# First expert of a mixture-of-experts stage: slots dealt to its tiles in turns, their read issued after one weight split, its transposes moved into the first step

## The chip, the cores and the metric

The kernel runs on one core of one Trainium2 chip. The metric is the device time of one execution in microseconds. A profiled execution also gives a span, from its first to its last instruction.

## The reference, cut to what matters

One transformer layer for 1024 tokens of 1024 columns: an attention mixer, then a mixture of 32 experts of which each token takes four. The part that the change touches:

```python
top_logits, top_e = lax.top_k(logits, TOP_K)           # 4 of 32 experts for each token
slot_tok = jnp.full((n_slots,), T).at[dest].set(flat_tok[order])
slot_w = jnp.zeros((n_slots,)).at[dest].set(top_w.reshape(-1)[order])
...
gu = xe @ w_gu[e] + b_gu[e]                            # xe: the tokens of expert e, 1024 -> 2048
x_glu = jnp.minimum(gu[:, :D_FF], SWIGLU_LIMIT)
x_lin = jnp.clip(gu[:, D_FF:], -SWIGLU_LIMIT, SWIGLU_LIMIT)
act = (x_lin + 1) * (x_glu * jax.nn.sigmoid(SWIGLU_ALPHA * x_glu))
return act @ w_dn[e] + b_dn[e]                         # 1024 -> 1024
...
y = jnp.zeros((T + 1, D)).at[slot_tok].add(yb * slot_w[:, None])
```

## The kernel before

The mixer ends with a router. For every token tile it writes pairs of (token, weight) into a DRAM table `slots_d` with indirect DMAs (L1295, issued by GpSimd). Each expert has a stretch of that table, and its slots lie one after the other.

The experts are then ranked by how many tokens they have, and the expert of rank r gets a fixed capacity `CAPS[r]`: 304, 280, 256, 224, 216, 208, 200, 184, 184, 176, 160, 160, 152, 144, 144, 136, then 128 fourteen times, and 64 twice. `positions()` puts the wide ones (capacity over 128) on even positions p = 0, 2, ... 30 in falling order, and the others between them. Position 0 has 304 slots, position 2 has 280, position 30 has 136, and position 31 has 128.

An expert at position p is worked on so. `slots(p)` (L1530) reads its part of `slots_d` into SBUF. `gather(p)` (L1546, GpSimd) fetches the token rows of 4 KB from DRAM, one indirect DMA for each tile of up to 128 slots. `xtr(p)` queues, for each tile and each half of the columns, a small chain `one`: four TensorE transposes (L1601), a rounded copy by ScalarE (`put_hi`, L1585) and the remainder by VectorE (`put_lo`, L1588). The weights come in pieces of 128x1024 (512 KB, `load`, L1493, on SyncE's queue). ScalarE and VectorE split each piece into a high and a low part (`split_hi` L1505, `split_lo` L1514). Steps "U" (four for the up projection) and "D" (two for the down projection) of four pieces each do the matmuls. Behind the last D step each tile of results is added to DRAM `f_d` with an accumulating indirect DMA (`scatter`, L1841, GpSimd). All of them add to the same `f_d`, so each waits until the one before it has landed.

Buffers: six for raw pieces, eight high parts, seven low parts, three for gathered tiles (`xg`), two PSUM tiles for transposes (`t5`). The steps follow one list, `steps`. Between pieces `slot()` runs: it advances the queued chains (`hot`, `cold`), then splits and loads one further piece. `need` advances chains until the halves that a step wants are done. Ahead of the first step, `prepare(0)` queues the transposes of position 0, a loop drains all of them, and only then the remaining splits and the steps follow. `prepare(p)` also reads the slots of p + 2 and queues the gather of p + 1, so GpSimd's queue holds gathers and scatters in one order.

Of the kernel before, what the change touches and what calls it, by code (L numbers as in the profile page):

```python
# [18 lines left out]
P = 128  # L19
# [7 lines left out]
def f(ap):  # L27
    return ap.bitcast(F32)
# [938 lines left out]
STRIDE = 1152  # L967
# [474 lines left out]
class Moe2(Tail):  # L1442
    def moe(self):
        nc, A, tc = self.nc, self.A, self.tc
# [18 lines left out]
        for p in range(NE):  # L1463
            c = caps[posr[p]]
# [3 lines left out]
        def ereg(eng, p):  # L1468
            r = posr[p]
            if (eng, p) not in regs:  # L1470
                regs[eng, p] = getattr(nc, eng).value_load(self.erow[0:1, r:r + 1], min_val=0, max_val=31)
            return regs[eng, p]
# [12 lines left out]
        def load(n=1, eng="sync"):  # L1485
            for _ in range(n):
                if st["l"] >= len(pieces):
                    return
                k, p, j, q = pieces[st["l"]]
                e = ereg(eng, p)  # L1490
                r = rawp.tile([P, 1024], F32, name="raw5")
                src = A["w_gu" if k == "U" else "w_dn"]
                getattr(nc, eng).dma_start(r, src[ds(e, 1), j * 4 + q].rearrange("a p c -> p (a c)"))  # L1493
                raws[st["l"]] = r
                st["l"] += 1

        def split_hi(n=1):
            for _ in range(n):
                i = st["h"]
                if i >= len(pieces):  # L1500
                    return
                while i not in raws:
                    load()
                his[pieces[i]] = hi = hip.tile([P, 1024], F32R, name="hi5")
                ACT.activation(hi, raws[i], AF.Copy)  # L1505
                st["h"] += 1

        def split_lo(n=1):
            for _ in range(n):
                i = st["s"]  # L1510
                if i >= len(pieces):
                    return
                los[pieces[i]] = lo = lop.tile([P, 1024], F32R, name="lo5")
                V.tensor_tensor(out=lo, in0=raws.pop(i), in1=f(his[pieces[i]]), op=ALU.subtract)  # L1514
                st["s"] += 1
# [3 lines left out]
        todo = {}  # L1519

        def tiles(p):
            c = caps[posr[p]]
            return [(a, min(P, c - a)) for a in range(0, c, P)]

        def slots(p, eng="sync"):
            if p >= NE:
                return
            e, nt = ereg(eng, p), len(tiles(p))
            sl = xgp.tile([P, 3, 2], I32, name="slot", bufs=8)
            getattr(nc, eng).dma_start(sl[:, :nt], self.slots_d[ds(e * STRIDE, nt * P), :].rearrange("(a p) c -> p a c", p=P))  # L1530
            SL[p] = [sl[:, i] for i in range(nt)]

        def columns(p):

            if p < NE and mode[p] == "T":
                b = xgp.tile([P, 24], F32, name="bcol", bufs=3)
                nc.sync.dma_start(b, A["b_col"][ds(ereg("sync", p), 1)].rearrange("a p c -> p (a c)"))
                BC[p] = b

        def gather(p):  # L1540
            if p >= NE:
                return
            XG[p] = []
            for (a, n), sl in zip(tiles(p), SL[p]):
                xg = xgp.tile([P, D], F32, name="xg")
                G.indirect_dma_start(out=xg[:n], out_offset=None, in_=self.h2_d,  # L1546
                                     in_offset=bass.IndirectOffsetOnAxis(ap=sl[:n, 0:1], axis=0))
                XG[p].append(xg)
# [10 lines left out]
        chains = deque()  # L1559
        hot, cold = deque(), deque()  # L1560

        def start(g):
            if next(g, chains) is not chains:
                chains.append(g)

        def advance():
            for _ in range(len(chains)):
                start(chains.popleft())
            q = hot or cold
            if q:  # L1570
                start(q.popleft())
# [19 lines left out]
        def xtr(p):  # L1591

            if p >= NE:
                return
            X[p], off = xalloc(p, "x")
            x = X[p]

            def one(a, n, xg, g):
                ps = tps.tile([P, 4, P], F32, name="t5")
                for i in range(4):  # L1600
                    T.transpose(ps[:, i, :n], xg[:n, (g * 4 + i) * P:(g * 4 + i + 1) * P], self.ident[:n, :n])  # L1601
                put_hi(ps[:, :, :n], g * 4, 4, a, n, x)
                yield
                put_lo(ps[:, :, :n], g * 4, 4, a, n, x, off)
                if mode[p] == "S" and n < 64:
                    G.memset(f(x[:, g * 4:g * 4 + 4, n:64]), 0.0)
                    G.memset(f(x[:, g * 4:g * 4 + 4, 64 + n:P]), 0.0)
                todo["U", p, g] -= 1

            ts = list(zip(tiles(p), XG.pop(p)))  # L1610
            for g in range(2):
                todo["U", p, g] = len(ts)
                for (a, n), xg in ts:
                    cold.append(one(a, n, xg, g))
            if mode[p] != "T":
                oh = wk.tile([P, P], F32R, name="oneh", bufs=2)
                G.memset(f(oh[64:P]), 0.0)
                V.tensor_copy(oh[0:64], self.R[:, posr[p]:posr[p] + 1].to_broadcast([64, P]))
                if mode[p] == "S":
                    V.tensor_copy(oh[0:64, 64:P], self.zeros[:64, 0:64])  # L1620
                OH[p] = oh
# [222 lines left out]
        def prepare(p):  # L1844

            if p >= NE:
                return
            slots(p + 2)
            columns(p + 2)
            xtr(p)  # L1850

            def then():
                gather(p + 1)
                return
                yield
            cold.append(then())
# [8 lines left out]
        for i in range(3):  # L1865
            cs = slice(i * D, i * D + D)
            ACT.activation(bhl[0:64, cs], rb[:64, cs], AF.Copy)
            V.tensor_tensor(out=bhl[32:64, cs], in0=rb[32:64, cs], in1=f(bhl[32:64, cs]), op=ALU.subtract)
        for i in range(4):
            split_hi()  # L1870
            split_lo()
            load()
            if i == 2:
                slots(0, "scalar")
                gather(0)
                slots(1, "scalar")
                G.memset(f(bhl[64:P]), 0.0)
        prepare(0)
        while cold or chains:
            advance()  # L1880
        split_hi(4)
        split_lo(3)
        for k, p, j in steps:
            (step_U if k == "U" else step_D)(p, j)
            if (k, p, j) == ("U", 0, 0):
# [187 lines left out]
```

## Time and profile before

| what | value |
|---|---|
| median of three runs | 2809.72 us (2807.43 to 2810.39) |
| the profiled execution's own time | 2805.38 us |
| its span | 2803.8 us |
| TensorE busy | 2667.9 us, 95% of the span |
| VectorE, ScalarE, GpSimd busy | 1959.0, 1591.8, 569.2 us |
| mean busy share of the DMA engines, expert stage | 0.67 to 0.93 by stretch |

The profiled execution spends 1.6 us outside its span, and it is 4.3 us below the median of the runs. Times in rows are microseconds from the start of the span. The expert stage begins at about 1162 and ends at about 2769.

### The profile page before, as it was taken

The numbers are of one execution on the slowest core, as the hardware profiler recorded it, in microseconds if no ns is written. First come the engines' busy times: TensorE is split into PE (matmuls) and PEld (weight loads), VectorE is DVE, ScalarE is ACT, GpSimd is POOL, SyncE is SP. The second block draws the span as 40 slices with busy tenths as digits, with TensorE's granted clock in tenths as the row PEclk, the third lists the DMA queues.
The fourth block names the chain that finished last, engine by engine and source line by source line (L and its number), as shares of the span: only waits on it lengthen the run. The fifth ranks groups of instructions, "written<-read, shape, count | busy, mean of one in ns | idle before, by whom it ended". The sixth has DMA issues, their size and how long they took to land. (4 is left out here: it accounts for less than half of the span.)

```text
span 2803.8 us, 44121 instructions
## 1 busy us (share of the span) xinstructions
PE 2667.9 (95%) x15564; PEld 2232.2 (80%) x15564; DVE 1959.0 (70%) x3148; ACT 1591.8 (57%) x2486; POOL 569.2 (20%) x492
## 2 busy tenths in 40 slices
PE   6999999999999999599999999999999999999993
PEld 4788887455677778499988899999989898999892
DVE  3722332777777546577877887888888888888895
ACT  3421211555577325356666666777777777777773
POOL 2310001665644232401010011011001100111001
PEclk9999999999999999699999999999999999999996
DMA  6225560502132343467787888898889889998896
GB/s 237 73 95 178 186 201 38 169 15 50 40 69 64 113 145 128 156 220 234 261 275 246 278 291 266 276 295 295 267 292 307 292 285 308 315 309 298 304 312 224
DMA packets 196608, 589.37 MB, mean 210 GB/s; under 512 B 49168, under 2 KB 55904, under 8 KB 196240
## 3 DMA queue, kind: packets, MB, share of 16 engines
q1 hardware_dynamic: 173424, 521.43, 55.5%
q0 software_dynamic: 19376, 63.70, 8.4%
q8 instruction: 123, 2.02, 0.3%
q10 hardware_dynamic: 3584, 1.40, 0.2%
q14 instruction: 101, 0.83, 0.1%
HBM read 528.75 MB, written 59.00 MB: 210 GB/s over the span
## 5 line engine op out<-in xcount | busy, mean ns | idle before, releaser
L1514 DVE TENSOR_TENSOR lo<-raw,hi 128x1024 fp32r<-128x1024 f32 x768 | 920.4, 1221 | 166.6 <-ACT hi L1505 67.9
L1505 ACT ACTIVATE hi<-raw 128x1024 fp32r<-128x1024 f32 x768 | 800.7, 1055 | 187.4 <-PE g L1669 85.6
L1669 PE MATMUL g<-xT,hi 128*128 128x320 f32 (+10 forms) x1792 | 518.6, 331 | 0.0
L1670 PE MATMUL g<-xT,lo 128*128 128x256 f32 x1792 | 483.7, 280 | 0.0
L1669 PEld LDWEIGHTS g<-xT,hi 128*128 128x128 f32 x1792 | 336.6, 188 | 10.9
L1670 PEld LDWEIGHTS g<-xT,lo 128*128 128x128 f32 x1792 | 338.4, 189 | 2.6
L1841 POOL DMA_INDIRECT f_d<-y,slot x34 | 61.1, 1797 | 1243.5 <-ACT y L1829 1103.9
L1669 PE MATMUL g<-aT,hi 128*128 128x288 f32 (+10 forms) x896 | 260.4, 333 | 0.0
L1670 PE MATMUL g<-aT,lo 128*128 128x256 f32 x896 | 241.8, 280 | 0.0
L1645 PE MATMUL g<-hi,xN 128*128 128x512 f32 x512 | 204.3, 399 | 0.0
L1646 PE MATMUL g<-lo,xN 128*128 128x512 f32 x512 | 203.3, 397 | 0.0
L174 DVE TENSOR_TENSOR wlo<-raw,whi 128x1024 fp32r<-128x1024 f32 x33 | 42.1, 1289 | 219.0 <-ACT whi L173 218.8
L1644 PE MATMUL g<-hi,xN 128*128 128x512 f32 x448 | 183.0, 408 | 0.0
L1669 PEld LDWEIGHTS g<-aT,hi 128*128 128x128 f32 x896 | 168.3, 188 | 5.2
L1670 PEld LDWEIGHTS g<-aT,lo 128*128 128x128 f32 x896 | 169.1, 189 | 0.7
L859 ACT ACTIVATE p<-S 128x512 f32<-128x512 f32 x160 | 94.2, 596 | 103.8 <-PE S L858 99.0
L613 DVE TENSOR_REDUCE mn<-S 128x1 f32<-128x512 f32 x180 | 100.9, 595 | 66.4 <-PE S L612 66.0
L400 PE MATMUL mm<-hTh,whi 128*128 128x512 f32 (+1 forms) x416 | 123.7, 385 | 1.7 <-ACT whi L173 1.7
L400 PE MATMUL mm<-hTh,wlo 128*128 128x512 f32 (+1 forms) x416 | 123.2, 383 | 0.0
L400 PE MATMUL mm<-hTl,whi 128*128 128x512 f32 (+1 forms) x416 | 123.0, 383 | 0.0
L1646 PEld LDWEIGHTS g<-lo,xN 128*128 128x128 f32 x512 | 96.8, 189 | 22.7
L1645 PEld LDWEIGHTS g<-hi,xN 128*128 128x128 f32 x512 | 97.0, 189 | 19.3
(414 smaller groups left out, 5807.9 us busy)
## 6 DMA issues: line engine op xcount, KB each, us to landing
raw<-in_w_gu_dram SPq DMA_DIRECT2D x512, 512.0 KB, 5.2
raw<-in_w_dn_dram SPq DMA_DIRECT2D x256, 512.0 KB, 4.4
raw<-in_w_mod_dram SPq DMA_DIRECT2D x40, 512.0 KB, 4.3
raw<-in_w_in_dram SPq DMA_DIRECT2D x34, 512.0 KB, 4.7
x<-in_x_dram SPq DMA_DIRECT2D x16, 512.0 KB, 4.9
sig_d<-stg POOLq DMA_DIRECT2D x16, 512.0 KB, 2.9
sig<-sig_d SPq DMA_DIRECT2D x8, 1024.0 KB, 5.0
kraw<-ka_d SPq DMA_DIRECT2D x16, 320.0 KB, 6.9
```

Of the source, the lines that this page charges most:

```text
L174: (G if i == 0 else V).tensor_tensor(out=lo, in0=r, in1=f(hi), op=ALU.subtract)
L400: T.matmul(ps[:, :n], w[:, ks], h[:, k, a:a + n], start=k == 0 and pi == 0, stop=k == KT - 1 and pi == 2)
L613: nc.vector.tensor_reduce(out=u.mn[:, i, j:j + 1], in_=ps[:, :n], op=ALU.min, axis=AX.X)
L859: nc.scalar.activation(u.p[t // 2][:, t % 2 * 512:t % 2 * 512 + 512], ps, AF.Exp, scale=-1.0)
L1505: ACT.activation(hi, raws[i], AF.Copy)
L1514: V.tensor_tensor(out=lo, in0=raws.pop(i), in1=f(his[pieces[i]]), op=ALU.subtract)
L1644: T.matmul(ps[:m], x[:, kk, P:P + m], hi[:, cs], start=False, stop=False)
L1645: T.matmul(ps[:m], x[:, kk, :m], hi[:, cs], start=False, stop=False)
L1646: T.matmul(ps[:m], x[:, kk, :m], lo[:, cs], start=False, stop=kk == 7)
L1669: T.matmul(ps[:, :2 * c], hi[:, cs], x[:, kk, :], start=first, stop=False)
L1670: T.matmul(ps[:, :256], lo[:, cs], x[:, kk, :256], start=False, stop=last)
L1841: G.indirect_dma_start(out=self.f_d, out_offset=bass.IndirectOffsetOnAxis(ap=SL[p][xi][:n, 0:1], axis=0), in_=Y[p][xi][:n], in_offset=None ...
```

## The change

It makes three edits.

1. `tiles(p)` no longer cuts the capacity c into tiles of 128 and a rest, but into t = ceil(c / 128) tiles whose sizes differ by one at most. 304 slots were 128, 128, 48 and become 102, 101, 101. 280 were 128, 128, 24 and become 94, 93, 93. The other wide ones were 128 and a rest and become two halves: 128 (as before), 112, 108, 104, 100, 92, 92, 88, 80, 80, 76, 72, 72 and 68.
2. `slots(p)` deals slots to the tiles in turns: slot s goes to partition s // t of tile s % t. For each partition the read then is one run of 8 t bytes instead of t runs of 8 bytes.
3. Ahead of the first step the loop runs seven times instead of four. The slot read, the gather of position 0 and the slot read of position 1 are issued after the first split instead of after the third. An eighth `split_hi` stands ahead of `prepare(0)`, and the drain is gone, so that the transposes of position 0 run where the first step asks for them.

```diff
         def tiles(p):
+
             c = caps[posr[p]]
-            return [(a, min(P, c - a)) for a in range(0, c, P)]
+            t = -(-c // P)
+            ns = [(c - i + t - 1) // t for i in range(t)]
+            return [(sum(ns[:i]), ns[i]) for i in range(t)]

         def slots(p, eng="sync"):
             if p >= NE:
                 return
-            e, nt = ereg(eng, p), len(tiles(p))
+            e, nt, n = ereg(eng, p), len(tiles(p)), tiles(p)[0][1]
             sl = xgp.tile([P, 3, 2], I32, name="slot", bufs=8)
-            getattr(nc, eng).dma_start(sl[:, :nt], self.slots_d[ds(e * STRIDE, nt * P), :].rearrange("(a p) c -> p a c", p=P))
+            getattr(nc, eng).dma_start(sl[:n, :nt].rearrange("p a c -> p (a c)"),
+                                       self.slots_d[ds(e * STRIDE, n * nt), :].rearrange("(p a) c -> p (a c)", a=nt))
             SL[p] = [sl[:, i] for i in range(nt)]
...
-        for i in range(4):
+        for i in range(7):
             split_hi()
             split_lo()
             load()
-            if i == 2:
+            if i == 0:
                 slots(0, "scalar")
                 gather(0)
                 slots(1, "scalar")
                 G.memset(f(bhl[64:P]), 0.0)
+        split_hi()
         prepare(0)
-        while cold or chains:
-            advance()
-        split_hi(4)
-        split_lo(3)
         for k, p, j in steps:
```

## Rows read from the trace of the kernel before

**Rows 1.** Busy time by stretch: PE, PEld, DVE, ACT, POOL, PE clock, DMA share, GB/s
```profile
1200.00:1300.00 100.00, 97.90 (x649) 92.18 (x649) 75.02 (x104) 56.83 (x76) 2.33 (x2) 0.98 0.67 214
...
2400.00:2600.00 200.00, 199.70 (x1308) 181.71 (x1307) 174.12 (x237) 150.58 (x225) 25.92 (x20) 1.00 0.93 310
```

**Rows 2.** Timeline, start of the expert stage: start, duration, engine, line, instruction, [idle before]
```profile
1165.26 1.04 POOL L1295 DMA_INDIRECT slots_d<-data,sl  x1 [0.22 <-issue]
...
1167.28 1.06 ACT L1505 ACTIVATE hi<-raw 128x1024 fp32r<-128x1024 f32 x1 [1.73 <-DMA raw<-in_w_gu_dram]
...
1171.57 1.62 ACTq L1530 DMA_DIRECT2D slot<-slots_d  x2
...
1173.24 1.06 ACT L1505 ACTIVATE hi<-raw 128x1024 fp32r<-128x1024 f32 x1 [1.60 <-DVE lo L1514]
...
1179.19 0.99 POOL L1546 DMA_INDIRECT xg<-h_d,slot  x1 [12.90 <-DMA slot<-slots_d]
```

**Rows 3.** Landing: the last table write of 1165.26, then position 0's slot read
```profile
DMA to landing us min/median/max: 6.1/6.1/6.1
...
slot<-slots_d ACTq DMA_DIRECT2D x1, 3.0 KB, 6.7
```

**Rows 4.** Timeline of PE: position 0's first transposes and first matmul
```profile
1183.92 1.09 PE L1601 MATMUL t<-ident,xg 128*128 128x128 f32 x4 [20.03 <-DMA xg<-h_d,slot]
...
1191.94 0.62 PE L1672 MATMUL g<-xT,hi 128*128 128x304 f32 x1
```

**Rows 5.** Queue packets: 1179-1187, 1217.9-1218.7, 1932-1944, 2762.3-2769.3 (all q0), 1164-1178 (q1)
```profile
q0 software_dynamic: 352, 1.25, 49.7%
...
q0 software_dynamic: 48, 0.10, 31.5%
...
q0 software_dynamic: 336, 1.05, 33.1%
...
q0 software_dynamic: 144, 0.52, 50.4%
...
q1 hardware_dynamic: 1473, 4.87, 96.1%
```

**Rows 6.** Busy time, columns of Rows 1: last scatter alone on the DMA engines
```profile
2766.00:2768.00 2.00, 0.00 (x0) 0.00 (x0) 0.00 (x0) 0.00 (x0) 0.00 (x0) 0.50 0.89 176
```

**Rows 7.** Timeline of POOL: position 0's three scatters, gather 4, position 2's first scatter
```profile
1303.06 1.92 POOL L1841 DMA_INDIRECT f_d<-y,slot  x1 [35.61 <-ACT y L1829]
1312.84 2.32 POOL L1841 DMA_INDIRECT f_d<-y,slot  x1 [7.86 <-DMA f_d<-y,slot]
1322.68 1.50 POOL L1841 DMA_INDIRECT f_d<-y,slot  x1 [7.52 <-ACT hi L1505]
...
1324.57 1.82 POOL L1546 DMA_INDIRECT xg<-h_d,slot  x1 [0.16 <-issue]
...
1412.64 1.87 POOL L1841 DMA_INDIRECT f_d<-y,slot  x1 [77.94 <-ACT y L1829]
```

**Rows 8.** Landing of the scatter of 1303.06
```profile
DMA to landing us min/median/max: 9.0/9.0/9.0
```

**Rows 9.** Timeline of PE: first transposes of positions 4 and 6
```profile
1370.45 0.60 PE L1601 MATMUL t<-ident,xg 128*128 128x128 f32 x4
...
1480.36 0.60 PE L1601 MATMUL t<-ident,xg 128*128 128x128 f32 x4
```

**Rows 10.** Tail: POOL timeline of position 30's two scatters, chain of waits for 31's
```profile
2747.16 1.77 POOL L1841 DMA_INDIRECT f_d<-y,slot  x1 [64.44 <-ACT y L1829]
2758.51 1.36 POOL L1841 DMA_INDIRECT f_d<-y,slot  x1 [9.57 <-issue]
...
2762.36 6.38 DMA f_d<-y5n,slot
```

**Rows 11.** Timeline of PE: position 30's transposes, 128 slots and 8
```profile
2629.12 0.60 PE L1601 MATMUL t<-ident,xg 128*128 128x128 f32 x4
...
2631.05 0.41 PE L1601 MATMUL t<-ident,xg 8*128 8x8 f32 x4
```

## The prediction, on record before the kernel was changed

> **What bounds the kernel now.** I read the busy time by stretch first. From 1200 to 1300 PE is busy 97.9 us of 100, from 2400 to 2600 199.7 of 200, while DVE and ACT have room [rows 1]. So the expert stage runs at PE's pace. Time moves if PE starts its first step at another time, if PE is made to wait inside, or if the tail behind PE changes.
>
> Then the timeline of the start. The last write of the slot table is issued at 1165.26 [rows 2] and lands 6.1 us later, at 1171.4 [rows 3]. The slot read is issued at 1171.57 [rows 2] and lands 6.7 us later [rows 3]; the first gather follows at 1179.19 [rows 2]. PE transposes from 1183.92 and has its first matmul at 1191.94 [rows 4].
>
> Last, GpSimd's timeline and the DMA queue's packets, because the change cuts new tile sizes, and gathers and scatters move one 4 KB row for each slot of a tile.
>
> **How a tile's rows are dealt to the DMA engines.** This decides the case, so it comes first. The last scatter has 128 rows and sends 144 packets [rows 5]: 16 besides its rows. The three gathers of position 0, 128 + 128 + 48 = 304 rows, send 352: 16 each besides. But the gather of 24 rows sends 48, so 8 too many. From 1932 to 1944 one scatter of 72 rows and gathers of 128 and 56 (256 rows, 1.05 MB) send 336: 80 beyond their rows, 32 more than three times 16 [rows 5].
>
> One dealing explains these counts: the rows go evenly to as many engines, up to 16, as divide their number, and each engine left over gets as many empty packets as a used one gets rows. 24 rows go two each to 12 engines, and 4 engines get 2 empty ones: 8. 72 go six each to 12: 4 x 6 = 24. 56 go four each to 14: 2 x 4 = 8, and 24 + 8 = 32. Dealing 72 rows to nearly all engines, five each, leaves 15 engines with at most five and would have sent 8 empty packets for 72, 16 in all instead of 32.
>
> The sizes before all share a factor of 8 or more, so at least 8 engines work. Of the new ones 101 is prime: one engine has all 101 rows. 102 gives 6 engines of 17 rows, 94 two of 47, 93 three of 31, 92 four of 23, 76 four of 19, 68 four of 17. The rest (112, 108, 104, 100, 88, 80, 72) have at least 10 engines and cost nothing, as a busiest engine has 10 rows at most, against 8 before.
>
> The Trainium skill states this for the descriptor generators ("DMA: Bandwidth & Descriptors", section "Why a DMA increments its semaphore by 16 and not by 1"): the number of engines is the largest up to 16 that divides the slowest dimension, and 127 partitions get one engine. The counts above agree with it. It also names an exception in which some copies issued by GpSimd spread over nearly all engines; by that the sum below would be that of the first rival, and no count here shows it for an indirect transfer.
>
> **What a row costs one engine.** A gathered row: 31.5% of 16 engines x 0.8 us over 24 rows is 0.168 us; in the three first gathers 49.7% x 16 x 8 us / 304 = 0.209 us. A weight row: 96.1% x 16 x 14 us over 4.87 MB / 4 KB = 1189 rows, 0.181 us [rows 5]. An accumulated row: 50.4% x 16 x 7 us / 128 = 0.44 us [rows 5], and in the middle of that scatter 0.89 x 16 x 2 us / 86 rows = 0.33 us [rows 6]. The scatter took 6.38 us [rows 10] with 8 rows on each engine, so 3 us are fixed. Beside the weights it is 9.0 us [rows 8]: (9.0 - 3) / 8 = 0.75 us. I take 0.55 (0.33 and one weight row between, an estimate), bounds 0.33 and 0.75.
>
> **The start.** The earlier place of the slot read is worth nothing: it needs the table write of 1171.4, so its issue stays, and ACT's splits two to eight queue behind it from 1173 on instead of two of them running before. They end at about 1181, under the gather. Larger runs may land the read earlier; of its 6.7 us I take 2 (0 to 4). The gathers then go out at 1177.2, 1178.5 and 1179.8, as close as now. A gather has 4.7 us from issue to PE with 8 rows per engine [rows 2, 4], so 3 us without rows. The third tile needs 101 rows on one engine: 17.0 us at 0.168. That engine also serves the six weight loads let through meanwhile, 48 rows x 0.181 = 8.7 us. So it lands at 1179.8 + 3 + 25.7 = 1208.5. Bounds: 1200 with no weights between, and 1234 if the two tiles of 101 meet on one engine at 0.209. With 2.5 us for transposes and their copies PE's first matmul comes at 1211 instead of 1191.94: 19 us late.
>
> The removed drain gives less than it looks. Six groups took 8.0 us [rows 4]. Three now stay ahead of the first matmul with a fourth beside them; the last two come between matmuls, about 0.5 us of PE each, and the last makes PE wait about 1.5 us for its two copies. 2.5 us come back: +21.5 for the start (+11 to +46).
>
> **The scatters of position 0.** They are issued at 1303.06, 1312.84 and 1322.68, each behind the landing of the one before, and the gather for position 4 stands behind them in GpSimd's queue, at 1324.57 [rows 7]. PE wants it at 1370.45 [rows 9], 67.4 us after the first scatter. Now: 102 rows, 17 on an engine, 3 + 17 x 0.55 = 12.4 us; then 101 rows on one engine, 3 + 55.6 = 58.6; then 58.6 again. The gather is issued just after the third's issue, but its rows queue behind the third's on that engine, so it lands at 12.4 + 58.6 + 58.6 + 3 = 132.6. PE waits 65 us. Bounds: at 0.33 8.6 + 36.3 + 36.3 + 3 = 84, a wait of 17; at 0.75 177, a wait of 110.
>
> **Position 2.** 47, 31 and 31 rows: 28.9 + 20 + 20 + 3 = 72 us, against 67.7 from 1412.64 to the transposes at 1480.36 [rows 7, 9]. That is 4 us of waiting; with weight pieces delayed on those engines I take 8 (0 to 26).
>
> **Other positions.** 92 (twice) and 76 add 22 to 30 rows to their busiest engines, at some 0.4 us more than a free one: 10 us of delay for pieces, mostly under the pieces split ahead. I take 4 (0 to 10).
>
> **The tail.** Position 30's scatters start at 2747.16 and 2758.51, and 31's behind them at 2762.36 [rows 10]: 11.3 us for 128 rows, 3.9 for 8. With 68 rows on four engines both have 17: the first 3 + 17 x 0.6 = 13, the second, alone, 3 + 17 x 0.38 = 9.5. That is +7.5 (+2 to +10).
>
> **What is gained.** Four transposes of 128 columns take 0.60 us and of 8 columns 0.41 [rows 11], so an expert with a small rest wins at most 0.2 us per half. Over the wide ones I take -1.5 (-3 to 0). Evacuations scale with columns, whose sum stays; the slot reads of later positions are done long before use.
>
> **Sum.** 21.5 + 65 + 8 + 4 + 7.5 - 1.5 = +104.5 us (+27 to +202 with all bounds at once). On the profiled execution's 2805.4 that is 2910; the median stood 4.3 above it, inside what I can tell.
>
> **Rivals.**
> First, rows are dealt evenly whatever their number. For it: no tile before is odd or prime, so nothing shows such a number. Against it: 336 packets [rows 5]. Then the start gains: tiles land 2 to 3 us earlier, two of six groups leave the front, 4.6 us in all, less the 2.8 that come back between matmuls: -1.8; with -1.5 of transposes and about -1 at the tail (11.3 falls more than 3.9 grows) 2801, no slower. It decides if a 101-row gather lands within about 6 us of its issue, so with some 15 rows on its busiest engine at most. Chance 0.10: faster by over 0.2% in 0.04, within in 0.06. (0.2%, 5.6 us, is about what a measurement of this kernel tells from no change.)
>
> Second, only the gathers bind: scatters on one engine run near 0.33 us and the gather for position 4 lands by 1390. For it: 15 engines stand free beside. Then 21.5 + 17 + 0 + 0 + 4 - 1.5 = +41: 2846. Chance 0.17.
>
> Third, the weights bind: pieces come at the pace of the engine that holds the scatter, 8 rows x (0.33 + 0.181) = 4.1 us each, where a pair of positions needs about 2, and PE starves beyond the waits above: +150 or more, 2955 and up. For it: DMA at 0.93 late [rows 1]; against it: some 13 pieces lie split or loaded ahead. Chance 0.15.
>
> **How the numbers follow.** The likeliest case, chance 0.56, is the sum: 2910, with 2865 to 2960 of its own. The second and third rivals lie on the same side. The range 2835 to 2990 holds the main case, the second rival and most of the third; what is left out is the first rival and the far end. Slower by over 0.2%: 0.56 + 0.17 + 0.15 = 0.88; same 0.07 and faster 0.05, with 0.02 left for a mishap in either.
>
> **What would show it.** The slot read still at about 1171.5; PE's first transposes of the second and third tiles 20 us behind the first's; scatters of position 0 spaced by some 12, then 60 us; a PE wait of tens of us on xg ahead of position 4's transposes; packet counts for 101 rows far above 117, as 15 engines get 101 empty ones. A first matmul before 1192, or scatters 10 us apart, would make it wrong.

## The result, and the profile after

The changed kernel takes 2945.66 us (median of 5 runs, 2940.51 to 2949.09) against 2809.72 before: ratio 1.0485, 95% interval 1.0471 to 1.05, slower. The profiled execution took 2940.51 us with a span of 2938.6, 134.8 us more than before's. In the changed kernel the lines named here have numbers larger by 4 (scatter L1845, gather L1550, transposes L1605).

The head of the page: busy time, then the span in 40 slices, then all packets, then the queue of the gathers and scatters; below it that queue before the change.

```profile
PE 2681.7 (91%) x15564; PEld 2248.6 (77%) x15564; DVE 1961.3 (67%) x3148; ACT 1591.7 (54%) x2486; POOL 580.1 (20%) x492
...
PE   6999999999999996695879999999999999999992
...
DMA packets 207386, 589.44 MB, mean 201 GB/s; under 512 B 59946, under 2 KB 66682, under 8 KB 207018
...
q0 software_dynamic: 33264, 63.78, 8.6%
```
```profile
q0 software_dynamic: 19376, 63.70, 8.4%
```

PE does the same 15564 matmuls and is busy 13.8 us longer. The rest is idle time, and the row of PE shows most of it in slices 16 to 21, around the start and behind it (before, slice 17 alone is low there). The bytes stay, and queue q0 sends 13888 packets more: the empty ones. Packets under 512 B grow by less, from 49168 to 59946, because the slot reads, in larger runs, send fewer (3110 on the other queues).

Now where in the span. For each even position I took the time of its first scatter [rows 7] and subtracted the same time before:

| first scatter of | 0 | 2 | 4 | 10 | 12 | 14 | 18 | 24 | 30 | last scatter |
|---|---|---|---|---|---|---|---|---|---|---|
| later by, us | 17.5 | 68.2 | 88.4 | 88.1 | 94.8 | 102.7 | 110.4 | 117.2 | 125.9 | 135.5 |

So the start takes 17.5 us more, position 0's stretch 50.7, position 2's 20.2, those of 4 to 28 together 37.5, and the tail 9.6.

The start, in the timelines of PE and GpSimd (start, duration, engine, line, instruction, idle time before it and what ended it):

```profile
1163.58 1.05 POOL L1295 DMA_INDIRECT slots_d<-data,sl  x1 [0.23 <-issue]
1175.65 1.99 POOL L1550 DMA_INDIRECT xg<-h_d,slot  x1 [11.02 <-DMA slot<-slots_d]
1177.95 3.04 POOL L1550 DMA_INDIRECT xg<-h_d,slot  x1 [0.30 <-issue]
1181.30 2.19 POOL L1550 DMA_INDIRECT xg<-h_d,slot  x1 [0.31 <-issue]
```
```profile
1189.38 0.91 PE L1605 MATMUL t<-ident,xg 102*128 102x102 f32 x4 [27.16 <-DMA xg<-h_d,slot]
1204.25 1.82 PE L1605 MATMUL t<-ident,xg 101*128 101x101 f32 x8 [13.96 <-DMA xg<-h_d,slot]
...
1207.04 0.60 PE L1676 MATMUL g<-xT,hi 128*128 128x304 f32 x1
```

From the last table write to the first matmul it is 43.5 us instead of 26.7 [rows 2, 4]. PE transposes the tile of 102 rows at 1189.4 and then stands another 14 us for the tiles of 101.

Position 0's scatters in GpSimd's timeline, and then PE's first wait in that stretch:

```profile
1320.58 2.07 POOL L1845 DMA_INDIRECT f_d<-y,slot  x1 [35.95 <-ACT y L1833]
1334.52 4.26 POOL L1845 DMA_INDIRECT f_d<-y,slot  x1 [11.87 <-DMA f_d<-y,slot]
1385.29 3.98 POOL L1845 DMA_INDIRECT f_d<-y,slot  x1 [46.52 <-DMA f_d<-y,slot]
1387.50 2.00 POOL L1621 MEMSET oneh<- 64x128 f32 x1
1389.66 1.02 POOL L1550 DMA_INDIRECT xg<-h_d,slot  x1 [0.17 <-issue]
...
1435.91 1.48 POOL L1845 DMA_INDIRECT f_d<-y5n,slot  x1 [43.97 <-DMA f_d<-y,slot]
```
```profile
1389.55 0.80 PE L1640 MATMUL g<-bhl,oneh 128*128 128x512 f32 x1 [36.41 <-POOL oneh L1621]
```

From each scatter to the next it is 13.9, 50.8 and 50.6 us (102, 101 and 101 rows), against 9.8 and 9.8 before [rows 7]. PE waits 36.4 us, but for something the prediction didn't name. A memset of the one-hot rows for the bias (L1621) also stands in GpSimd's queue behind the scatters, and the bias matmul of an earlier step wants it before position 4's transposes want their rows. What else the 50.7 us hold is 11.5 us of shorter waits (1.9 before), 7.5 of them for VectorE's `gx` (the activation between the two projections), and 4.5 us by which PE's own work takes longer at a granted clock of 0.85 on the mean instead of 0.98. The waits of PE from 1160 to 2900 (total us, times, longest) show it at the head:

```profile
PE g L1640 <- POOL oneh L1621: 56.8, 2, 36.4
PE t L1605 <- DMA xg<-h_d,slot: 42.6, 4, 27.2
PE t L1711 <- DVE gx L1705: 33.3, 9, 7.5
```

The second of the two waits for the one-hot tile is 20.4 us, behind position 2's scatters. The third of them, the memset behind it, and PE:

```profile
1528.33 2.21 POOL L1845 DMA_INDIRECT f_d<-y,slot  x1 [18.25 <-DMA f_d<-y,slot]
1529.64 1.12 POOL L1621 MEMSET oneh<- 64x128 f32 x1
```
```profile
1530.81 0.80 PE L1640 MATMUL g<-bhl,oneh 128*128 128x512 f32 x1 [20.40 <-POOL oneh L1621]
```

How few DMA engines work meanwhile, first by stretch (columns of [rows 1]), then in the queue's packets from 1336 to 1386, in which one scatter of 101 rows ran:

```profile
1370.00:1380.00 10.00, 0.00 (x0) 0.00 (x0) 0.00 (x0) 0.00 (x0) 0.00 (x0) 0.50 0.07 17
```
```profile
q0 software_dynamic: 1632, 0.43, 5.8%
```

A share of 0.07 is one engine of 16 (0.0625), every compute engine is idle, and PE's granted clock is at the lower level (0.50, 1.2 GHz). 1632 packets are 101 rows, 16, and 15 idle engines with 101 empty packets each. The empty ones are gone early: from 1345 to 1384 the queue sent 87 packets at that pace of one engine.

### The profile page after: what moved, and what is told of

Its sections match the earlier page's. It is cut to its first block, busy times and chain, and to the rows that moved or that the text cites. A ratio compares the mean times of both kernels' runs of the same rounds, so it can differ in the third digit from the quotient of the medians.

```text
span 2938.6 us, 44131 instructions
## 1 busy us (share of the span) xinstructions
PE 2681.7 (91%) x15564; PEld 2248.6 (77%) x15564; DVE 1961.3 (67%) x3148; ACT 1591.7 (54%) x2486; POOL 580.1 (20%) x492
## 2 busy tenths in 40 slices
DMA packets 207386, 589.44 MB, mean 201 GB/s; under 512 B 59946, under 2 KB 66682, under 8 KB 207018
## 5 line engine op out<-in xcount | busy, mean ns | idle before, releaser
L1673 PE MATMUL g<-xT,hi 128*128 128x320 f32 (+10 forms) x1792 | 529.1, 336 | 2.5 <-DVE gx L1751 2.5
L1674 PE MATMUL g<-xT,lo 128*128 128x256 f32 x1792 | 490.8, 284 | 0.0
L1673 PEld LDWEIGHTS g<-xT,hi 128*128 128x128 f32 x1792 | 343.7, 192 | 14.4 <-DVE gx L1751 3.8
L1674 PEld LDWEIGHTS g<-xT,lo 128*128 128x128 f32 x1792 | 345.4, 193 | 2.4
L1845 POOL DMA_INDIRECT f_d<-y,slot x34 | 70.8, 2082 | 1290.4 <-ACT y L1833 1050.6
```

Of the source, the lines that this page charges most:

```text
L1673: T.matmul(ps[:, :2 * c], hi[:, cs], x[:, kk, :], start=first, stop=False)
L1674: T.matmul(ps[:, :256], lo[:, cs], x[:, kk, :256], start=False, stop=last)
L1845: G.indirect_dma_start(out=self.f_d, out_offset=bass.IndirectOffsetOnAxis(ap=SL[p][xi][:n, 0:1], axis=0), in_=Y[p][xi][:n], in_offset=None ...
```

## The experiments

Each kernel was run beside the kernel before on the same chip; its median there was 2808.4 to 2808.9. The stretches are as above: start, position 0, position 2, positions 4 to 28, tail.

| kernel | median us | ratio, interval | start | 0 | 2 | 4-28 | tail |
|---|---|---|---|---|---|---|---|
| changed | 2945.66 | 1.0485, 1.0471 to 1.05 | 17.5 | 50.7 | 20.2 | 37.5 | 9.6 |
| A: tiles in multiples of 8 | 2823.47 | 1.0054, 1.004 to 1.0069 | 11.8 | -1.2 | -0.7 | 7.7 | 0.8 |
| B: order alone | 2808.2 | 1.0002, 0.9993 to 1.0011 | -0.3 | 0.1 | -2.0 | 0.8 | 0.6 |
| C: tiles and reads alone | 2946.63 | 1.0495, 1.0478 to 1.0512 | 18.5 | 52.0 | 21.0 | 39.9 | 9.9 |
| D: gathers padded to 16 | 2916.47 | 1.0391, 1.0374 to 1.0408 | 5.5 | 52.0 | 21.3 | 20.0 | 9.5 |
| E: position 0 alone dealt | 2877.96 | 1.0242, 1.0227 to 1.0258 | 24.3 | 52.1 | -2.0 | -0.8 | -0.1 |
| F: memset on VectorE | 2935.88 | 1.0451, 1.0435 to 1.0467 | 16.6 | 48.7 | 8.4 | 44.2 | 9.8 |
| G: sizes of before, dealt in turns | 2808.5 | 1.0001, 0.9992 to 1.001 | 2.2 | 0.1 | -2.0 | 0.4 | 0.7 |
| H: 184, 152, 136 in halves | 2856.73 | 1.0167, 1.0151 to 1.0183 | 4.1 | 0.0 | -2.0 | 39.5 | 9.9 |
| I: A, position 0 by 16 | 2821.04 | 1.0044, 1.0032 to 1.0056 | 4.7 | -1.2 | -0.2 | 11.5 | 0.8 |
| J: A, 152 to 136 as before | 2815.46 | 1.0022, 1.0012 to 1.0031 | 8.2 | -1.2 | 0.4 | 3.1 | 0.6 |

The column "start" also holds how late the work ahead ended. The last table write fell between 1162.12 (B) and 1170.16 (E) in these profiles, though the code ahead of it is the same, so a few us of that column belong to no edit.

**A, B, C and D: which of the edits, and by which transfers.**

A cuts every position into multiples of 8 rows (304 = 104 + 104 + 96); where the tiles of a position differ in size, the list is read in two DMAs. All else is the changed kernel.

```diff
-            ns = [(c - i + t - 1) // t for i in range(t)]
+            u = c // 8
+            ns = [(u - i + t - 1) // t * 8 for i in range(t)]
```

> The changed kernel with tile sizes in multiples of 8 (304 = 104 + 104 + 96, 280 = 96 + 96 + 88, 184 = 96 + 88, 152 = 80 + 72, 136 = 72 + 64 and so on), so that the busiest engine has 9 rows at most. Dealing theory: the whole loss goes, 2803 to 2813 us, the scatters of position 0 about 10 us apart, PE's first matmul between 1186 and 1192. Rival (the order of the start, or the reads by larger runs, cost by themselves, or balanced tiles load the DMA engines more): 2825 or more.

B is the kernel before with the new order of the start alone, C has the new tiles and reads with the old order (the diff's last hunk taken or left).

> The kernel before with the new order of the start alone (seven splits, slot read after the first, no drain), tiles of 128 and a rest, reads in runs of 8 bytes. Dealing theory: no loss, 2804 to 2811 us, first matmul 1 to 4 us earlier than 1191.94 and about 2.5 us of that given back between the first matmuls. Rival (the weight loads now beside the gather hold it up): first matmul later than 1192, 2812 to 2820.

> The new tiles and slot reads alone, with the old order of the start (slot read after the third split, all transposes drained ahead of the first step). Dealing theory: about as slow as the changed kernel, 2938 to 2952 us, since the tiles of 101 rows decide when the first step starts. Rival (the new order makes part of the loss): 2925 or less.

D is the changed kernel, but each gather fetches rows up to the next multiple of 16 (the surplus rows are not used), and the slot read is padded likewise; scatters keep their sizes.

```diff
+                m = -(-n // 16) * 16
-                G.indirect_dma_start(out=xg[:n], out_offset=None, in_=self.h2_d,
-                                     in_offset=bass.IndirectOffsetOnAxis(ap=sl[:n, 0:1], axis=0))
+                G.indirect_dma_start(out=xg[:m], out_offset=None, in_=self.h2_d,
+                                     in_offset=bass.IndirectOffsetOnAxis(ap=sl[:m, 0:1], axis=0))
```

> The changed kernel, its scatters unchanged, but each gather fetches rows up to the next multiple of 16 (112 for 101 and 102, 96 for 92 to 94, 80 for 76 and 68), the slot read likewise; the extra rows are not used. Dealing theory: the late start goes (18 us), the waits of 51 and 20 us behind the scatters of positions 0 and 2 and the 10 us at the tail stay, and of the 38 us at later positions about half: 2895 to 2922 us. Rival (the gathers make the loss, scatters come after them): 2815 to 2835.

C alone gives the whole loss and B none of it, so the order is worth nothing that shows and the tiles are all. A, with the same number of tiles and the same work but sizes that share a factor of 8, loses 14.8 us instead of 136. That is between the two expectations: most of the loss is the dealing, and 15 us stayed open (I and J). D moves more rows and is 29 us faster: its start falls from 17.5 to 5.5 and three stalls go, while positions 0 and 2 and the tail, where scatters are what waits, stay. Its transposes of the tiles of 101 wait 2.15 us and 1.56 us instead of 13.96:

```profile
1188.04 0.91 PE L1607 MATMUL t<-ident,xg 102*128 102x102 f32 x4 [24.32 <-DMA raw<-in_w_gu_dram]
1191.10 0.94 PE L1607 MATMUL t<-ident,xg 101*128 101x101 f32 x4 [2.15 <-DMA xg<-h_d,slot]
1193.59 1.58 PE L1607 MATMUL t<-ident,xg 101*128 101x101 f32 x8 [1.56 <-DMA xg<-h_d,slot]
```

**E and H: does each loss belong to its own sizes?** E cuts and deals position 0 alone, H only the capacities 184 (twice), 152 and 136; all other positions have 128 rows and a rest. Both have the new order; H also deals every position's slots in turns and reads a list in up to two DMAs.

```diff
+            if p > 0:
+                return [(a, min(P, c - a)) for a in range(0, c, P)]
```

and in H

```diff
+            if c not in (184, 152, 136):
+                return [(a, min(P, c - a)) for a in range(0, c, P)]
```

> The new order and the new reads, but only position 0 is cut into 102, 101 and 101 rows; every other position keeps tiles of 128 rows and a rest. Theory (each position's loss belongs to its own tile sizes): the start's 19 us and the 51 us of position 0 stay, what follows keeps step with the kernel before, so about 2809 + 19 + 51 = 2879 us, 2870 to 2888. Rival (the later losses are only what an upset start leaves behind): steps at positions 2 and 10 to 28 and at the tail stay too, and the time is 2920 to 2946.

> The new order and the sizes of the kernel before, except that the positions of capacity 184, 152 and 136 are cut into halves of 92, 76 and 68 rows, which divide by 4 and not by 8. Theory (the 38 us lost between positions 10 and 28 and the tail's part come from exactly these sizes): about 2808 + 38 + up to 9 = 2850 us, 2840 to 2862. Rival (these losses come only because position 0 had delayed everything before): 2808 to 2818 us.

Both theories held. E has the start and 52.1 us at position 0, and from there on keeps step with the kernel before. H has none of that and loses 39.5 us in positions 4 to 28 and 9.9 at the tail, as the changed kernel does (37.5 and 9.6). So the losses add up by position, and the late ones don't need an upset start. (E and H together lose 118 us of the 137 or so; position 2 alone was not run.) In H PE's largest waits from 1300 on are eight for VectorE's `gx` (27.7 us). The stretch from position 10's first scatter to position 12's, in which position 14's tiles of 92 are gathered, in the kernel before, in H and in the changed kernel:

```profile
1824.34:1923.04 98.70, 98.26 (x583) 90.22 (x582) 82.12 (x108) 69.33 (x101) 10.38 (x7) 1.00 0.87 283
```
```profile
1826.40:1931.38 104.98, 100.51 (x584) 92.33 (x583) 81.83 (x108) 69.25 (x101) 9.68 (x8) 0.97 0.84 266
```
```profile
1912.48:2017.85 105.37, 100.47 (x584) 92.33 (x583) 81.97 (x108) 69.13 (x101) 10.41 (x7) 0.97 0.83 265
```

Of the 6.7 us that this stretch grows in the changed kernel, 2.2 are PE's own work, which takes longer: part of it ran at the lower of the two clock levels (a mean of 0.97; 0.75 from 1959.5 to 1970, behind the stall, and 1.00 from 1970 on). The chain behind that stall, in the timelines of ScalarE and PE and in the waits of ScalarE over the stretch:

```profile
1941.37 1.06 ACT L1505 ACTIVATE hi<-raw 128x1024 fp32r<-128x1024 f32 x1 [6.62 <-DMA raw<-in_w_gu_dram]
```
```profile
1959.52 0.69 PE L1711 MATMUL t<-ident,gx 128*128 128x128 f32 x2 [3.70 <-DVE gx L1705]
```
```profile
ACT hi L1505 <- DMA raw<-in_w_gu_dram: 9.2, 3, 6.6
```

Before, ScalarE waited 1.5 us once for such a piece in that stretch; in H it is 9.6 us in four waits. The two tiles of 92 are asked for at 1924.63 and 1926.85. ScalarE gets the late piece at 1941.37, VectorE makes up for the late splits in between its other work, and PE stands for VectorE's `gx` until 1959.52. That this is one chain is read from the timelines; that the sizes start it is what H shows, and D, with the gathers padded, has no stall in this stretch.

**F: the memset moved.** The changed kernel with the memset of the one-hot rows on VectorE.

```diff
-                G.memset(f(oh[64:P]), 0.0)
+                V.memset(f(oh[64:P]), 0.0)
```

> The changed kernel with one edit: the memset of the one-hot rows is VectorE's instead of GpSimd's, so it no longer stands behind the scatters of position 0 and 2. Theory (PE waits first for the memset, but the gather of position 4 stands behind the same scatters and lands little earlier than PE needs it): the two waits of 56.8 us for the one-hot tile vanish from the profile, a wait for the rows of position 4 takes the place of most of the first one, and of the 20 us at position 2 most goes: about 2925 us, 2912 to 2935. Rival (the memset is the only thing that holds PE there): about 2946 - 57 = 2889 us, 2880 to 2900.

The waits for the one-hot tile are gone and the time falls by 10 us, not 57; it ended 1 us above the theory's range, and positions 4 to 28 lose 44.2 us where they lost 37.5, which no run explains. In position 0's stretch the wait that the prediction named stands in its place (PE's timeline):

```profile
1381.09 0.47 PE L1711 MATMUL t<-ident,gx 64*128 64x64 f32 x2 [14.96 <-DVE gx L1705]
...
1436.81 1.12 PE L1605 MATMUL t<-ident,xg 128*128 128x128 f32 x4 [31.31 <-DMA xg<-h_d,slot]
```

The rows of position 4 come 117 us behind the first scatter (1319.67), whatever PE waits for first. At position 2, 12 of the 20 us go: there the memset was the cause of that part. What is left is 8.4, and in it PE waits 5.8 us for VectorE's `gx` and 2.5 us for its `xT`, and none for gathered rows.

**G: turns and reads without the sizes.** The new order, slots dealt in turns and read by larger runs (a list in up to two DMAs, as in A), tiles of 128 and a rest.

> The new order and the new way of dealing slots to tiles in turns, read by larger descriptors, with the tile sizes of the kernel before (128 rows and a rest); each list is read in up to two DMAs. Theory (the sizes alone cost time; turns and larger reads are worth nothing that shows): 2804 to 2812 us. Rival (the dealing in turns or the reads carry the 15 us that the tiles in multiples of 8 left): 2820 us or more.

No difference that can be told, as the theory had it. So edits 2 and 3 are worth nothing, and the 15 us of A are its sizes. B and G are as fast as the kernel before; none of these kernels is faster.

**I and J: what A still lost.** I is A with position 0 in 112, 96 and 96 rows; J is A with 152, 144 and 136 cut as before.

```diff
-            ns = [(u - i + t - 1) // t * 8 for i in range(t)]
+            ns = {304: [112, 96, 96]}.get(c) or [(u - i + t - 1) // t * 8 for i in range(t)]
```

and in J

```diff
-            ns = [(u - i + t - 1) // t * 8 for i in range(t)]
+            ns = {152: [P, 24], 144: [P, 16], 136: [P, 8]}.get(c) or [(u - i + t - 1) // t * 8 for i in range(t)]
```

> The kernel with all tiles in multiples of 8 rows, with one edit: position 0 is 112, 96 and 96 rows (multiples of 16) instead of 104, 104 and 96. From the last table write to the first matmul it took 30.9 us there, 26.7 in the kernel before. Theory (104 rows are 13 engines' work, 8 rows each, and three engines stand idle): that stretch becomes 27 to 28 us, the late loss of about 8 us stays, and the time is 2816 to 2822 us. Rival (the start waits for something else, as three tiles in turns that all must land): the stretch stays above 30 us, and the time is 2821 or more.

> The kernel with all tiles in multiples of 8 rows, with one edit: the positions of capacity 152, 144 and 136 are cut into 128 rows and a rest of 24, 16 and 8 as in the kernel before, instead of 80 and 72, 72 and 72, 72 and 64. Theory (its late 8 us belong to the 72-row tiles, 12 engines' work): positions 24 to 30 and the tail keep step with the kernel before, the start's loss of about 4 us stays, and the time is 2812 to 2817 us. Rival (the 8 us come of the larger sizes ahead, 88 and 104 rows): it stays at 2820 or more.

Last table write to first matmul is 28.6 us in I, against 30.9 in A and 27.4 in B and G: 2.3 of A's 3.5 us over B belong to the 104 rows, though I's theory had 27 to 28. The time of I, 2821.0, lies where both expectations touch and tells nothing. In J the stalls of positions 24 to 30 and the tail are gone (1.2 us in all instead of 8), but one of 3.1 us stands at position 10, where A had 1.1. In I stalls of 3 to 5 us stand at positions 14, 18 and 24, with the same sizes as A from position 2 on. One of them, from position 18's first scatter to position 20's (before: 91.68 us, PE busy 91.57):

```profile
2217.48:2314.55 97.07, 93.65 (x583) 85.78 (x582) 79.50 (x108) 67.99 (x101) 8.54 (x7) 0.96 0.87 286
```

So with tiles that 11 to 13 engines work on (88, 72 and 104 rows) a stall sometimes comes, at places that move from kernel to kernel. ScalarE's waits for pieces, from position 10's first scatter to position 30's, grow in all of these kernels: 17.6 us before, 39.6 in J, 52.9 in A and I, 78.2 in the changed kernel. Most of that is covered: A loses 7.7 us there. Which size does it, and why there, stays open.

## Why the prediction was right in sign and near in size

2945.7 against 2910, inside the range; the likeliest case held. That the total came this near is in part luck: the loss was forecast too high by 18 us at the start and position 0, and too low by 46 at position 2 and the others. By its steps:

**The dealing held, to the packet.** At the start 304 rows, 3 x 16, 10 idle engines x 17 for the 102 and 2 x 15 x 101 for the tiles of 101 make 3552 packets; from 1175.5 to 1207 the queue sent just that:

```profile
q0 software_dynamic: 3552, 1.26, 22.0%
```

The stretch of position 10 above has 648 rows in six transfers (two scatters of 104, two gathers of 92, one of each kind of 128), so 648 + 96 packets and the empty ones: two of 104 (3 idle x 8 each) and two of 92 (12 idle x 23 each) are 48 + 552 = 600, in all 1344. Before, the tile of 56 alone gave any (2 idle x 4), so 752. The queue's rows of the changed kernel and of the kernel before:

```profile
q0 software_dynamic: 1344, 2.66, 11.4%
```
```profile
q0 software_dynamic: 752, 2.65, 11.8%
```

Over the whole run the dealing gives 208 empty packets before and 14096 in the changed kernel, for all gathers and scatters together, and q0's growth, 13888, is exactly the difference. The first rival, rows dealt evenly, is out. So is the second, in which the scatters cost near 0.33 us a row and position 4's rows land by 1390, 87 us behind the first scatter: a row took about 0.44, and PE has those rows 117 us behind it.

The Trainium skill's rule ("DMA: Bandwidth & Descriptors", section "Why a DMA increments its semaphore by 16 and not by 1"), the largest number up to 16 that divides the slowest dimension, agrees with all of these packet counts; its exception for some direct copies of GpSimd doesn't show in any of these indirect transfers.

**The start: +21.5 predicted, 17.5 measured,** 19.2 if counted from the last table write. The first matmul is 16.8 us later against that write, where 19 was forecast. The 2.5 us that were to come back behind the first matmul did: 19.2 less 16.8 is 2.4. What failed is a part, shown by B, where the first matmul was expected 1 to 4 us earlier. It came 2.4 us earlier, but the last table write fell 3.1 earlier too; counted from that write the first matmul is 0.8 later, and position 0's first scatter 2.8 later (-0.3 and 3.1); B regains 2.0 in position 2's stretch. From its first gather to PE it takes 8.4 us where it took 4.7 [rows 2, 4], perhaps because more weights are let through ahead of it. From the first gather to the first transposes, B and then the kernel before:

```profile
1175.70:1184.10 8.40, 0.00 (x0) 0.02 (x1) 1.60 (x2) 1.06 (x1) 5.84 (x4) 0.50 1.02 398
```
```profile
1179.20:1183.90 4.70, 0.00 (x0) 0.01 (x1) 0.00 (x0) 0.00 (x0) 4.05 (x4) 0.50 0.58 170
```

The DMA share (second from the right) is full in the one and 0.58 in the other. That this is the reason is argued, not shown: the profile puts the end of PE's wait in B down to a weight piece. That the earlier place of the slot read gains next to nothing held: its issue, 1168.78, is 5.2 us behind the last table write of 1163.58; it was 6.3 [rows 2].

**Position 0: +65 predicted, 50.7 measured.** The place and the cause were right, two details weren't. The accumulated row was mis-sized: 0.55 us was taken between 0.33 (the second rival's price) and 0.75. Scatters of 17 rows on the busiest engine took 13.9 us, of 31 20.5 (the second such tile at most 17.0), of 47 27.0 and of 101 50.6, so about 6 us and 0.44 for each row, as in the last scatter of [rows 5]; with 13.9 + 50.8 + 50.6 for the forecast's 12.4 + 58.6 + 58.6 its 65 becomes 51. And PE waits for the one-hot memset first. F shows that this changes little here, as the rows of position 4 come late by nearly as much.

**Position 2: +8 predicted, 20.2 measured.** The step "what PE waits for is the gather" failed here. The memset comes earlier in PE's order and stands behind the third scatter all the same. With the memset elsewhere (F) the loss is 8.4. That this meets the forecast of 8 is in part luck: 4 of the 8 were a wait for gathered rows, and F has none there.

**Other positions: +4 predicted, 37.5 measured.** This is the term that was mis-sized most. It took a delay of 10 us for pieces and held it for mostly covered "under the pieces split ahead". The delay was far larger: ScalarE's waits for pieces between positions 10 and 30 grow from 17.6 to 78.2 us (75.1 in H), as a tile of 92, 76 or 68 rows is both gathered and scattered. And it isn't covered as far as that: part of each delay reaches PE by way of the split and VectorE, and PE then also works for a while at the lower clock (over these positions PE is busy 929.4 us instead of 920.6). In H they give 39.5 us by themselves.

**The tail: +7.5 predicted, 9.6 measured.** The two scatters take 14.9 and 9.9 us where 13 and 9.5 were forecast (2873.08, 2887.97, 2897.90).

**The third rival** (the weights bind everywhere) didn't come: from 1370 to 1380 the DMA engines stand at 0.07, so no piece was being loaded. Its mechanism, late pieces behind a few loaded engines, is by the chain read above what costs 37.5 us in the other positions.

The transposes' -1.5 can't be told from the rest.

## What to carry to other kernels

Cut indirect transfers so that their row count has a factor of 16, or at least 8 (A, with 8, still lost 14.8 us): equal halves or thirds can be far worse than a full tile and a rest. Look at the packets of the queue: here those beyond the rows and 16 for each transfer were idle engines times the rows of a busy one. And for a queue that waits, list all that stands behind the wait on that engine, memsets too, and ask which of it the bounding engine wants first.

## What the runs showed of the hardware that was not expected

Fetching more rows can be much faster: with 10 or 11 unused rows more for each tile, D's first matmul came 30.0 us behind the last table write instead of 43.5. The first rows of a gather came to PE after 8.4 us beside a full DMA load (B) and after 4.7 at a share of 0.58, so issuing it earlier, among more loads, gained nothing. A small memset behind a waiting scatter held PE for 36.4 us, yet moving it gave back only 10, as the rows behind the same scatter came late too. And a short stall costs more than itself: in position 10's stretch 2.2 of 6.7 us were PE's own matmuls, slower at a granted clock of 0.97 on the mean instead of 1.00.
